# New prices and latencies in a kernel's order planner, and TensorE bound to the planner's order

## The chip, the cores and the metric

One core of one Trainium2 chip runs the kernel. The metric is the time of one execution in microseconds (us) on the device; the time given for a kernel is the median of its runs. TensorE is called PE in the profile, its weight loads PEld, VectorE DVE, ScalarE ACT, GpSimd POOL, and SyncE, which only issues DMAs, SP.

## The reference, cut to what matters

One layer of a decoder in float32, for a prompt of 512 tokens and 8 samples of one token each, 520 columns in all. Both groups use the same weights (d = 1024, FFN 2816).

```python
def hybrid_mixer(h, ...):
    proj = h @ w_in                              # 1024 -> 10016
    a_cols, s_cols, gate_a, gate_b = split(proj)
    for g in 3 groups:                           # (window, dilation) = (128,1), (512,4), (2048,16)
        q, k = rope(q), rope(k)                  # 8 heads of 64
        o[g], lse[g] = dilated window attention(q, k, v)
    o_a = sum_g softmax_g(lse) * o[g]
    o_b = rwkv7_time_mix(s_cols, ...)            # 16 heads of 64
    merged = sigmoid(gate_a) * (o_a @ w_proj_a) + sigmoid(gate_b) * (o_b @ w_proj_b)
    return merged @ w_out

def rwkv7_time_mix(p, prev, wkv0):
    xm = p + (shifted(p) - p) * mu_shift
    r, k, v, xw, xa, xg = split(xm)
    decay, a, gate = lora(xw), lora(xa), lora(xg)
    S_t = S * w_t + (S @ -kk_t) (kk_t * a_t)^T + v_t k_t^T     # scan over the tokens
    y_t = S_t @ r_t
    yn = group_norm(y) * gn_w + gn_b             # one group per head
    return (yn + bonus) * gate

x = x + hybrid_mixer(rms_norm(x), ...)
x = x + (silu(hn @ w_gate) * (hn @ w_up)) @ w_down             # hn = rms_norm(x)
y = rms_norm(x)
```

The new keys, values and RWKV states are outputs too.

## The kernel before

**Tiling.** Activations lie with channels on the partitions, in 8 blocks k of 128, and the 520 columns in two halves ("chunks") of 260. A product in float32 is made of three fast ones: each operand is split into a high part, rounded to the short format, and the rest (`whi` and `wlo` for weights; `hh`, `hl` for the normalised input, `hu`, `lu` for the first job's; `mh`, `ml` for the merged heads, `fh`, `fl` and `h2h`, `h2l` in the FFN), and high x high, low x high and high x low are added in PSUM. So a block of 128 output channels, a "job", is 8 x 3 matmuls of 128x128 weights and 260 columns for each half.

**Main stream.** `play` (L549) goes through the jobs: the attention's q, k, v and the RWKV's r, k, v of w_in, the gates (`hh`, `hl`), the projection of the attention's result (inputs `tw`, `k`, `ta`, `r`, `v`, used again as buffers; result summed up in `ga`), that of the RWKV's result (`OB`), w_out (`mh`, `ml`), the FFN. It fetches a weight block (`raw`), and ScalarE and VectorE split it into `whi` and `wlo`, one job ahead.

**Side streams.** The rest is generators that are spawned as their inputs appear: rotary turns (`turn`), attention (`heads`), the samples' attention and RWKV, and for each of 8 pairs of heads `pair` (the mixing and the LoRA products, tiles `LW`, `LA`, `lw`), `solve`, `turn_a` and `chain` (L1355). A chain goes through 8 blocks of 64 tokens, a "step" each: 64x64 products into `ch` from `VTr`, `GH` and the state `AR`; two ScalarE copies of `ch` into `GH`; 64x64 products `GH`, `KB`; a VectorE update of `AR`. Behind the last step come the outputs y (30 small products, of `GH` and of `AR`), copied into `KB` by ScalarE. Then follows the GroupNorm (L1424 to L1465): means `gm`, squares `gq` on ScalarE, a reciprocal root in ten VectorE operations (`rsy`, `rst`, L592), a product into `KB`, and four 128x128 transposes on TensorE, `ax<-ident,KB`. The last pair's normalisation is made of VectorE operations of 512 columns in place of the eight small ScalarE ones.

**What sets the order.** Python runs the generators. `Weave.run` (L433) picks at each point, by a model of time (`Clocks`, L226), a side stream whose awaited tiles are ready by the clock of TensorE, or else the main stream. `Unit.price` (L336) gives each operation's duration, and `Clocks.run` (L300) its start: after its inputs, its output tile's earlier users, and the work placed on its engine before. A stream stops at `yield tiles` until these are ready in the model. That gives the order in which the program is written:

```python
                p = self.price(op, outs, ins)
                if self.name == "PE":
                    ...
                    t = self.ck.run(self.name, outs, ins, p if self.ck.hot else 2 * p)
                ...
            if TIMED:
                self.tc.cur_priority = int(t * TIMED)
            r = f(*a, **k)
            return self.keep(r) if self.keep else r
```

With `TIMED = 0` and `PIN = 0` that order isn't the final one: the framework's scheduler sorts the instructions of each engine again, by its own estimates of when each can start and with the written order as priority. All instructions are issued through `Unit.__getattr__` (L353), so nearly all of them carry line L380 in the profile (L420 in the changed kernel); tiles tell them apart.

**The norms.** `norm2` (L1761) is spawned behind the last job of w_out, and `final` (L1822) behind the last job of the FFN. Each begins with `norm_r` (L608), whose first operations are matmuls with a column of ones: they sum `accf` (squares of x summed over the blocks) over the partitions. Neither has a `yield` ahead of them.

## Time and profile before

| | |
|---|---|
| time, median of 3 runs | 1314.66 us (1313.83 to 1316.19) |
| the profiled execution | 1316.53 us |
| its span in the trace | 1314.8 us, mean granted TensorE clock 0.983 |
| busy: TensorE, weight loads, VectorE, ScalarE, GpSimd | 1264.7, 1197.5, 843.7, 610.6, 175.0 us |
| start (0 to 33) | TensorE busy 23.98 of 33 us |
| mixer (33 to 858) | 795.07 of 825 us |
| output projection and FFN (858 to 1287) | 428.87 of 429 us |
| end (1287 to 1314.8) | 16.80 of 27.8 us |

A row of a timeline is start, duration (both us), engine, line, operation, tiles out<-in, tile of the array, form and count; in brackets stands the engine's idle time before it and what ended that. Matmuls overlap in the records, so that the distance between starts, not the duration, is what one costs. A group's row is engine, operation, tiles, form, count | busy us, mean ns of one | idle before and what ended it.

### The profile page before, as it was taken

To read this page: it belongs to the slowest core of one execution; us is meant where nothing else is said; L and a number is where in the kernel's file an instruction comes from. 1 tells how busy PE (TensorE), PEld (TensorE's weight loads), DVE (VectorE), ACT (ScalarE), POOL (GpSimd) and SP (SyncE) were. 2 spreads that over 40 slices of the span, in tenths; PEclk is the share of its full clock that TensorE was granted. 3 is DMA by queue.
4 is the path that set the end of the run, shared out by engine and by line. 5 is a ranking of instruction groups with operands and counts; after the bars stand their busy time and mean duration, and the time that the engine had idled before them with its cause. 6 is when DMAs were issued, how large, how long until landed. Compare 5 with 4: busy or idle time off the path is not lost.

```text
span 1314.8 us, 29468 instructions
## 1 busy us (share of the span) xinstructions
PE 1264.7 (96%) x11738; PEld 1197.5 (91%) x11738; DVE 843.7 (64%) x2221; ACT 610.6 (46%) x1554; POOL 175.0 (13%) x261
## 2 busy tenths in 40 slices
PE   7999999999989989999999999999999999999996
PEld 7998999989978878888888888999999999999996
DVE  6956866954869998886986665555843444332333
ACT  5244244366656656675785665334433232222220
POOL 1300100100223332121123122110200000000000
PEclk9999999999989999997999999999999999999998
DMA  6523654634245554543245454552222222223331
GB/s 215 158 94 96 213 178 146 221 112 172 69 131 136 152 147 141 143 156 97 77 139 168 123 175 157 182 192 85 81 97 97 97 89 89 97 93 89 89 101 65
DMA packets 92137, 169.48 MB, mean 129 GB/s; under 512 B 42416, under 2 KB 47568, under 8 KB 92000
## 3 DMA queue, kind: packets, MB, share of 16 engines
q1 hardware_dynamic: 60880, 102.46, 24.6%
q0 software_dynamic: 14512, 46.47, 11.5%
q10 hardware_dynamic: 16608, 18.68, 4.3%
q8 instruction: 92, 1.51, 0.5%
q14 instruction: 45, 0.37, 0.1%
HBM read 133.20 MB, written 27.94 MB: 123 GB/s over the span
## 4 chain that ended last, share of the span: by engine, by line
PE 64%; DVE 15%; issue 9%; DMA 6%; ACT 4%; POOL 1%; SPq 1%; ACTq 0%; DVEq 0%; POOLq 0%
PE mm L380 51%; PE ax L380 8%; PE ch L380 5%; DVE wlo L380 2%; DVE X L380 1%; DVE xt L380 1%; DMA fb<-FD 1%; DMA sw<-raw 1%; ACT KB L380 1%; DVE k L380 1%; DMA raw<-w_in 1%; SPq L380 1%; DVE raw L380 1%; DVE qk L380 1%; DVE GH L380 1%
## 5 line engine op out<-in xcount | busy, mean ns | idle before, releaser
L380 PE MATMUL mm<-hh,whi 128*128 128x260 f32 x1136 | 340.2, 299 | 0.8 <-ACT gt L380 0.8
L380 PE MATMUL mm<-hh,wlo 128*128 128x260 f32 x1136 | 325.4, 286 | 4.3 <-DVE wlo L380 4.3
L380 PE MATMUL mm<-hl,whi 128*128 128x260 f32 x1136 | 325.7, 287 | 0.0
L380 ACT CAST whi<-raw 128x1024 fp32r<-128x1024 f32 (+1 forms) x165 | 170.1, 1032 | 324.4 <-PE mm L380 290.6
L380 DVE TENSOR_TENSOR wlo<-raw,whi 128x1024 fp32r<-128x1024 f32 (+1 forms) x165 | 197.9, 1199 | 140.2 <-ACT whi L380 137.0
L380 PEld LDWEIGHTS mm<-hh,whi 128*128 128x128 f32 x1136 | 215.7, 190 | 13.3 <-issue 6.0
L380 PEld LDWEIGHTS mm<-hh,wlo 128*128 128x128 f32 x1136 | 215.4, 190 | 6.5 <-DVE wlo L380 5.8
L380 PEld LDWEIGHTS mm<-hl,whi 128*128 128x128 f32 x1136 | 215.5, 190 | 1.4 <-issue 0.2
L380 PE MATMUL mm<-h2l,whi 128*128 128x260 f32 x608 | 171.5, 282 | 0.0
L380 PE MATMUL mm<-h2h,wlo 128*128 128x260 f32 x608 | 171.4, 282 | 0.0
L380 PE MATMUL mm<-h2h,whi 128*128 128x260 f32 x608 | 171.4, 282 | 0.0
L380 PEld LDWEIGHTS mm<-h2h,wlo 128*128 128x128 f32 x608 | 114.5, 188 | 0.0
L380 PEld LDWEIGHTS mm<-h2l,whi 128*128 128x128 f32 x608 | 114.4, 188 | 0.0
L380 PEld LDWEIGHTS mm<-h2h,whi 128*128 128x128 f32 x608 | 114.4, 188 | 0.0
L380 PE MATMUL mm<-fh,wlo 128*128 128x260 f32 x388 | 109.6, 282 | 0.0
L380 PE MATMUL mm<-fh,whi 128*128 128x260 f32 x388 | 109.5, 282 | 0.0
L380 PE MATMUL mm<-fl,whi 128*128 128x260 f32 x388 | 109.5, 282 | 0.0
L380 PEld LDWEIGHTS mm<-fh,whi 128*128 128x128 f32 x388 | 73.1, 188 | 0.0
L380 PEld LDWEIGHTS mm<-fl,whi 128*128 128x128 f32 x388 | 73.0, 188 | 0.0
L380 PEld LDWEIGHTS mm<-fh,wlo 128*128 128x128 f32 x388 | 72.9, 188 | 0.0
L380 DVE TENSOR_TENSOR xt<-X,LT 128x60 f32<-128x60 f32 (+24 forms) x248 | 60.3, 243 | 3.6
L380 DVE TENSOR_TENSOR X<-X,xt 128x60 f32<-128x60 f32 (+24 forms) x248 | 57.6, 232 | 3.8
(390 smaller groups left out, 2588.8 us busy)
## 6 DMA issues: line engine op xcount, KB each, us to landing
raw<-w_in SPq DMA_DIRECT2D x77, 512.0 KB, 3.7
raw<-w_gate SPq DMA_DIRECT2D x22, 512.0 KB, 3.2
raw<-w_up SPq DMA_DIRECT2D x22, 512.0 KB, 3.2
raw<-w_down SPq DMA_DIRECT2D x16, 512.0 KB, 3.5
kt<-kcache POOLq DMA_DIRECT2D x24, 256.0 KB, 3.7
kt<-vcache POOLq DMA_DIRECT2D x24, 256.0 KB, 3.5
sw<-raw ACTq DMA_DIRECT2D x64, 65.0 KB, 3.6
GD<-gt ACTq DMA_DIRECT2D x16, 260.0 KB, 3.0
```

The source lines that it names most:

```text
L380: r = f(*a, **k)
```

## The change

It has three parts. First, the planner's figures: every engine's prices, the latency by which a result reaches another engine (`HOP`, by the writing engine, in place of 0.2 for all), DMAs, a surcharge on TensorE when the tile shape changes (`shift`), and rules by which a tile can't be used before its pool's predecessor is closed and its older users are through. Second, some `yield`s of side streams wait for more tiles, and one of `norm0` goes. Third, the starts that the planner gives to TensorE's instructions are kept in `ck.log`; at the end they are sorted by start and each is tied to the one before by a dependency without a semaphore. So TensorE's order is now the planner's; the other engines' instructions are sorted by the framework's scheduler as before. The matmuls are the same in number and shape.

```diff
-TIMED = 0
-PIN = 0
-L_SEM = 0.2
+HOP = {"PE": 0.2, "DVE": 0.04, "ACT": 0.04, "POOL": 0.1, "SP": 0.03}
...
 class Clocks:
     def last(d, engine, r=None):
-        t = 0.0
+        t, wake = 0.0, 0.2 if engine == "POOL" else 0.03
...
-                t = max(t, end + (late if by != engine else 0.0 if by == "PE" else 0.12))
+                t = max(t, end + (late + wake if by != engine else 0.0))
...
     def free(self, name, engine, r=None):
-        if name not in self.done and name in self.prev:
-            name, r = self.prev[name], None
-        return max(self.last(d.get(name, {}), engine, r) for d in (self.done, self.used))
+        n = self.prev.get(name)
+        return max([self.floor.get(name, 0.0), self.begun.get(self.order.get(name), 0.0)] +
+                   [self.last(d.get(name, {}), engine, r) for d in (self.done, self.used)] +
+                   [self.last(d.get(n, {}), engine) for d in (self.done, self.used)])
...
+    def shift(self, shape, op):
+        wide, t = shape == (128, 128), 0.0
+        if shape != self.shape:
+            t = 0.19 if wide else 0.09
+        elif wide and self.turned and op != "transpose":
+            t = 0.09
+        self.shape, self.turned = shape, op == "transpose"
+        return t
...
 class Unit:
-            return 0.06 + n / 1200
+            return (0.23 if op == "activation" else 0.18) + n / 1200 + (0.19 if more else 0)
         if self.name == "POOL":
-            return 0.25 + n / 480
+            return 0.2 + n / (310 if outs[0].dtype == FR else 600)
         if self.name != "PE":
-            return 0.07 + n / 960
+            if op == "tensor_tensor_scan":
+                return 0.155 + n / 480
+            return 0.155 + n / 960 + (0.05 if op == "scalar_tensor_tensor" else 0.08 if more else 0)
...
-        if ins[0].dtype == FR:
-            return max(0.054, n / 2400)
...
+        elif ins[0].dtype == FR:
+            p = max(0.065, 0.0115 + n / 2400)
...
+        return p + self.ck.shift((rows, cols), op)
...
-                t = self.ck.run(self.name, outs, ins, (2.7 if pool else 1.6) + kb / 360, 1.04 if pool else 0.45, 0.8)
+                t = self.ck.run(self.name, outs, ins, (3.4 if pool else 2.7) + kb / 300, 0.56 if pool else 0.36, 0.03)
...
-            if TIMED:
-                self.tc.cur_priority = int(t * TIMED)
             r = f(*a, **k)
-            return self.keep(r) if self.keep else r
+            self.ck.log[self.name].append((t, len(self.ck.log[self.name]), r.ins))
+            return r
...
     def norm0():
             split(hh[:, k], hl[:, k], t[:], (V, G)[k % 2])
-            yield (hl[:, k],)
...
     def gates2():
-            yield lo, st3, BANK
+            yield hi, lo, st3, rw["XGh"], rw["XGl"], rw["XS"], BANK
...
     def pair(p):
-        yield lo, BANK
+        yield hi, lo, LW, BANK
...
-        yield (BANK,)
+        yield LA, BANK
...
     def merge():
+            yield stat, BANK
...
     wv.run(play(jobs, more))
     fctx.close()
+    for log in (ck.log["PE"],):
+        log.sort(key=lambda x: x[:2])
+        for (_, _, a), (_, _, b) in zip(log, log[1:]):
+            tc.add_manual_dep(b, a.name, mybir.DependencyInfo(mybir.DependencyClass.NoSync, mybir.DependencyReason.DATA),
+                              reason="order")
```

Three places of the orders follow. The number behind a tile's name is that of its allocation; it differs between the kernels.

**The end of the mixer, TensorE.** Before, the four transposes of the last pair's GroupNorm (KB_9763) stand among the last gate products (`hh`, `hl`), and the output products (`OB`) come next; 77 gate products stand between that pair's y and these transposes.

```order
L380 MATMUL mm_11567<-hh,wlo_11408 128x260
L380 MATMUL mm_11567<-hh,whi_11407 128x260
L380 MATMUL mm_11567<-hl,whi_11407 128x260
L380 MATMUL ax_11590<-ident,KB_9763 128x128 x4
L380 MATMUL mm_11567<-hh,wlo_11408 128x260
L380 MATMUL mm_11625<-OB_11289,whi_11544 128x260 x2
L380 MATMUL mm_11625<-OB_11289,wlo_11545 128x260
L380 MATMUL mm_11625<-OB_11349,whi_11544 128x260 x2
```

Now there are no gate products left. Behind two bare steps of the last pair (KB_10239) stand the transposes of the pair before it (KB_9468), and behind them the last pair's y.

```order
L420 MATMUL ch_11441<-AR_9818 64x64 x2
L420 MATMUL ch_11441<-GH_9906,KB_10239 64x64
L420 MATMUL ch_11441<-GH_9907,KB_10239 64x64
L420 MATMUL ch_11492<-VTr_10292,GH_9906 64x64
L420 MATMUL ch_11492<-VTr_10292,GH_9907 64x64
L420 MATMUL ch_11492<-AR_9818 64x64 x2
L420 MATMUL ch_11492<-GH_9906,KB_10239 64x64
L420 MATMUL ch_11492<-GH_9907,KB_10239 64x64
L420 MATMUL ax_11516<-ident,KB_9468 128x128 x4
L420 MATMUL ch_11525<-GH_9906 64x64
L420 MATMUL ch_11525<-GH_9907 64x64
```

Fourteen more rows like the last two and one of `AR` (14 products) follow, and then `OB`. The gate products moved ahead by some 460 places.

**The second norm, TensorE.** `accf` holds the sums of squares; `mm<-mh` are the last products of w_out, `ch<-fh` and `ch<-fl` the first ones of the FFN. Before, thirty of the FFN's products stand ahead of the sum over the partitions:

```order
L380 MATMUL ch_12699<-fl,whi_12625 128x260
L380 MATMUL ch_12699<-fh,wlo_12626 128x260
L380 MATMUL ch_12730<-fh,whi_12625 128x260
L380 MATMUL ch_12730<-fl,whi_12625 128x260
L380 MATMUL ch_12730<-fh,wlo_12626 128x260
L380 MATMUL ax_12679<-ones,accf 104x1 x5
L380 MATMUL ch_12730<-fh,whi_12625 128x260
L380 MATMUL ch_12730<-fl,whi_12625 128x260
```

Now the sum comes directly behind w_out's last product:

```order
L420 MATMUL mm_12641<-mh,wlo_12563 128x260
L420 MATMUL mm_12641<-mh,whi_12562 128x260
L420 MATMUL mm_12641<-ml,whi_12562 128x260
L420 MATMUL mm_12641<-mh,wlo_12563 128x260
L420 MATMUL ax_12679<-ones,accf 104x1 x5
L420 MATMUL ch_12699<-fh,whi_12625 128x260
L420 MATMUL ch_12699<-fl,whi_12625 128x260
L420 MATMUL ch_12699<-fh,wlo_12626 128x260
```

So the sum moved ahead of the FFN's products. The same happens at `final`, where nine products of the down projection stood ahead.

**A GroupNorm near the mixer's end, VectorE and TensorE.** KB_8458 is a pair's y, `rst` and `rsy` its reciprocal root. On TensorE now:

```order
L420 MATMUL mm_11219<-r_10327,wlo_11093 128x260
L420 MATMUL mm_11219<-r_10328,whi_11092 128x260
L420 MATMUL mm_11219<-v_10332,whi_11092 128x260
L420 MATMUL mm_11219<-r_10328,wlo_11093 128x260
L420 MATMUL ax_11235<-ident,KB_8458 128x128 x4
L420 MATMUL mm_11244<-tw_10325,whi_11209 128x260
L420 MATMUL mm_11244<-k_10329,whi_11209 128x260
```

On VectorE now, up to the split of a weight block; five more steps of the root and `KB<-KB,rsy` come behind:

```order
L420 TENSOR_TENSOR rst_11122<-rsy_11121 128x8
L420 SCALAR_TENSOR_TENSOR ga_11077<-ga_11077,mm_11219 128x260
L420 SCALAR_TENSOR_TENSOR rst_11122<-rst_11122,gv_11035 128x8
L420 TENSOR_TENSOR OB_11568<-ys,OB_11568 128x8
L420 TENSOR_TENSOR OB_11575<-ys,OB_11575 128x8
L420 SCALAR_TENSOR_TENSOR rsy_11121<-rst_11122,rsy_11121 128x8
L420 TENSOR_TENSOR rst_11122<-rsy_11121 128x8
L420 TENSOR_TENSOR wlo_11314<-raw_11257,whi_11313 128x1024
```

VectorE before, for the same pair of heads (KB_8264):

```order
L380 TENSOR_TENSOR rst_10946<-rsy_10945 128x8
L380 SCALAR_TENSOR_TENSOR AR_8762<-AR_8762,PC_8570,ch_11048 128x64
L380 SCALAR_TENSOR_TENSOR rst_10946<-rst_10946,gv_10895 128x8
L380 SCALAR_TENSOR_TENSOR AR_9464<-AR_9464,PC_9243,ch_11088 128x64
L380 SCALAR_TENSOR_TENSOR rsy_10945<-rst_10946,rsy_10945 128x8
L380 SCALAR_TENSOR_TENSOR ga_10931<-ga_10931,mm_11076 128x260
L380 TENSOR_TENSOR KB_8264<-KB_8264,rsy_10945 128x512
L380 SCALAR_TENSOR_TENSOR AR_8762<-AR_8762,PC_8570,ch_11103 128x64
```

`ga<-ga,mm_11219` needs the product that stands last ahead of the transposes on TensorE, and stands on VectorE ahead of the operations that these transposes need. Before, no operation between the root's steps needed a product so late on TensorE: the last `ga` ahead of `KB<-KB,rsy` used mm_11076, which ended some 20 rows ahead of the transposes.

**The start, TensorE.** The products of the first job's two halves (mm_195 and mm_226) were mixed as slices of x came in; now the 24 of the first half stand ahead of the 24 of the second.

## The prediction

> **What bounds the kernel now.** I read the first part of the page, the busy time by stretch, TensorE's waits, and then the timeline where something is priced.

> ```profile
> span 1314.8 us, 29468 instructions
> ...
> PE 1264.7 (96%) x11738; PEld 1197.5 (91%) x11738; DVE 843.7 (64%) x2221; ACT 610.6 (46%) x1554; POOL 175.0 (13%) x261
> ```

> The columns of the stretches are length, busy time of PE, PEld, DVE, ACT and POOL, the granted clock, the DMA share and GB/s.

> ```profile
> 33.00:858.00 825.00, 795.07 (x7845) 729.65 (x7845) 622.01 (x1855) 463.95 (x1340) 159.14 (x238) 0.98 0.47 143
> 858.00:1287.00 429.00, 428.87 (x3589) 428.38 (x3588) 188.80 (x281) 126.58 (x179) 12.11 (x14) 1.00 0.30 98
> 1287.00:1314.80 27.80, 16.80 (x146) 16.29 (x144) 10.84 (x40) 0.84 (x2) 0.00 (x0) 0.80 0.23 77
> ```

> TensorE bounds it. From 858 on (output projection and FFN) it is idle for 0.13 us of 429, so an order can only lose there. All that can be won lies in the mixer, 33 to 858, where PE idles 30 us; beside that, its work costs more or less with the neighbours that the order gives it. VectorE is busy 75% of that stretch (622 of 825), so it is a second queue that a late operation has to get through.

> TensorE's waits (what waits, for what, total us, times, longest) have 21 rows from 7.6 down to 0.3 us, 41.8 in sum:

> ```profile
> PE mm L380 <- ACT whi L380: 7.6, 3, 7.1
> PE mm L380 <- DVE wlo L380: 5.1, 6, 1.4
> PE ch L380 <- ACT GH L380: 4.0, 4, 2.4
> ...
> PE mm L380 <- ACT hu L380: 1.7, 1, 1.7
> ...
> PE ax L380 <- DVE AR L380: 0.3, 1, 0.3
> ```

> The longest whi wait (7.1) is the first matmul's and the hu wait (1.7) is the start's too. The other 33 us are many waits of about 1 us on side streams: weights just split, steps of the RWKV chain, transposes of things not yet normalised.

> **The change, part by part.** The edits to prices, latencies and pool times issue no instruction; they count only through the order. The matmuls are the same ones. So I compare the two orders.

> *Fewer changes of tile shape.* A 64x64 step put among 128-wide matmuls costs more than its work:

> ```profile
> 795.36 0.28 PE L380 MATMUL mm<-v,whi 128*128 128x260 f32 x1
> 795.57 0.33 PE L380 MATMUL ch<-VTr,GH 64*64 64x64 f32 x4
> 795.74 0.28 PE L380 MATMUL ch<-AR 64*64 64x64 f32 x4
> 795.95 0.38 PE L380 MATMUL mm<-r,wlo 128*128 128x260 f32 x1
> 796.17 0.28 PE L380 MATMUL mm<-r,whi 128*128 128x260 f32 x1
> ```

> Starts of 128-wide matmuls in a run lie 0.12 apart (17.22 and 17.34 below). Into the 64x64 group it is 0.21 (+0.09); the first 128-wide one after it comes about 0.10 late, and the next 0.22 after that (another +0.10). In the orders, entries fall from 167 to 126, returns from 150 to 108, and changes between two small shapes rise from 116 to 144, at about 0.1 each: -41 x 0.09 - 42 x 0.205 + 28 x 0.1 = **-9.5 us**. That is the surest term: TensorE pays it whatever the others do. Half of it remains if the profile's spacing overstates it.

> *The mixer's waits.* With trace durations the plan places a chain step later. The step's rows are these, with those of the GroupNorm that follows a pair's chain:

> ```profile
> L380 ACT ACTIVATE GH<-ch,DN 64x64 f32<-64x64 f32 x128 | 39.6, 309 | 25.2 <-PE ch L380 20.9 <-DMA BVD<-tmp 1.8 <-issue 0.6
> ...
> L380 ACT ACTIVATE gq<-KB,gm 128x64 f32<-128x64 f32 x56 | 19.4, 346 | 0.7
> ...
> L380 DVE SCALAR_TENSOR_TENSOR AR<-AR,PC,ch 128x64 f32<-128x64 f32 x56 | 15.5, 278 | 20.3 <-PE ch L380 12.7 <-ACT gq L380 2.9 <-ACT VTr L380 2.3
> ...
> L380 ACT ACTIVATE KB<-ch 128x64 f32<-128x64 f32 x56 | 11.6, 235 | 3.9 <-PE ch L380 3.9
> ...
> L380 ACT ACTIVATION_READ_ACCUMULATOR gq<-KB,gm 128x1 f32 x56 | 10.5, 188 | 0.0
> ...
> L380 DVE SCALAR_TENSOR_TENSOR ga<-ga,mm 128x260 f32<-128x260 f32 x16 | 6.8, 423 | 3.3 <-PE mm L380 3.3
> ...
> L380 DVE TENSOR_TENSOR KB<-KB,gm 128x512 f32<-128x512 f32 x8 | 5.5, 688 | 3.0 <-ACT gq L380 2.9
> ...
> L380 DVE SCALAR_TENSOR_TENSOR rsy<-rst,rsy 128x8 f32<-128x8 f32 (+1 forms) x27 | 4.5, 166 | 0.4
> ```

> Between a step's first products and its second, which need two GH copies (2 x 0.309), stood 5 to 12 wide matmuls (0.6 to 1.4 us); now 12 to 42 (1.4 to 5.0). Counting in both orders the places where less than 2 us of TensorE work is left over beyond the bare durations of what is awaited, I find 104 before and 63 now. All 33 us go into the sum as removed, and the new waits come in again: at 33 / 104 = 0.32 us for a tight place, 63 of them would cost 20. Worked out singly, six GroupNorm transposes stand too early, for 12 us together. The largest is the one shown in VectorE's order: the transposes of KB_8458 come straight after the last product of mm_11219, but ahead of their last input VectorE has ga<-ga,mm_11219 (0.42), then two small adds and eight steps of the reciprocal root (0.2 each with the gap) and the product (0.69): 3.1 us, and more if the split wlo between them is late. The others, by the same rows, are 1.0 to 2.9. I add 6 for the rest: **-33 + 18**, the 18 between 5 and 40.

> *The mixer's tail.* Before, 77 gate matmuls (9.2 us at 0.12) stood between the last chain and the output product OB. Now they were used up earlier. Of the last two pairs, the first (KB_9468) has its y products, then only two steps of the other pair (three groups of small products each, 0.2 a group as above: 1.2 us), then its transposes. From y to the transposes that pair needs 8 x 0.235 (copies) + 8 x (0.346 + 0.188) (squares) + ten root steps at 0.2 + 0.69 = 8.9 us. So TensorE stands 7.7 us, with the other pair's y behind it in its queue. The two shared steps ahead of that leave it idle for some 3, and the second pair's normalisation (five wide operations at 0.69, root steps 2.0, copies 0.6: 6.0) is covered by 48 OB products (5.8) but for up to 1.5, with up to 3 more for changes of shape and stragglers: 11.5 to 16, I take **+14**.

> *The second norm.* From the timeline of before:

> ```profile
> 916.99 0.28 PE L380 MATMUL mm<-mh,wlo 128*128 128x260 f32 x1
> ...
> 917.31 0.43 DVE L380 TENSOR_TENSOR x<-x,mm 128x260 f32<-128x260 f32 x1 [1.87 <-PE mm L380]
> ...
> 918.82 0.63 ACT L380 ACTIVATE sq<-x 128x520 f32<-128x520 f32 x1
> ...
> 920.13 0.69 DVE L380 TENSOR_TENSOR accf<-accf,sq 128x520 f32<-128x520 f32 x1
> ...
> 920.97 0.99 PE L380 MATMUL ax<-ones,accf 128*104 128x1 f32 x10
> ```

> Thirty products of the FFN (3.6 us) covered the way from the last output product through x, sq and accf to the sum over channels. They now stand behind it, so TensorE waits: 920.97 - 917.11 = **+3.9**; 3 if ScalarE does sq ahead of the cast. The last norm loses its cover likewise:

> ```profile
> 1290.48 0.28 PE L380 MATMUL mm<-fh,lw 128*128 128x260 f32 x1
> ...
> 1291.84 0.23 PE L380 MATMUL ax<-ones,sq 128*65 128x1 f32 x2
> ```

> 1291.84 - 1290.60 = **+1.2**.

> *The start.* The first job was taken by both halves as slices of x came in; now all 24 products of the first half come first.

> ```profile
> 7.11 0.58 PE L380 MATMUL mm<-hu,whi 128*128 128x260 f32 x1 [7.11 <-ACT whi L380]
> ...
> 16.06 0.64 PE L380 MATMUL mm<-hu,whi 128*128 128x260 f32 x2
> 16.49 0.42 PE L380 MATMUL mm<-lu,whi 128*128 128x260 f32 x1
> 16.71 0.42 PE L380 MATMUL mm<-hu,wlo 128*128 128x260 f32 x1
> ...
> 17.22 0.28 PE L380 MATMUL mm<-hu,wlo 128*128 128x260 f32 x1
> 17.34 0.28 PE L380 MATMUL mm<-hu,whi 128*128 128x260 f32 x1
> ```

> ```profile
> 15.52 0.75 DVE L380 SCALAR_TENSOR_TENSOR lu<-xt,feat,hu 128x520 fp32r<-128x520 f32 x1
> ```

> The last slice is there at 16.27, when 32 of the 48 products had begun; now 24 + 2 would still wait, ten more, at 0.12 to 0.22 each: 1.2 to 2.2, less if the second half catches up. **+1.5**.

> *The clock.* In 594 to 627 the granted clock was 0.74 though TensorE was busy 32.6 of 33 us:

> ```profile
> 594.00:627.00 33.00, 32.58 (x278) 29.09 (x277) 21.60 (x81) 19.79 (x50) 5.31 (x7) 0.74 0.28 85
> ```

> At half clock a wide matmul takes 0.22, not 0.12 (rows at 16.49 and 17.22), so 26% of 33 us at a reduced clock cost about 8 us over the 0.12 pace, if each slowed product lost 0.1. Longer runs of wide products should spare some: **-3**, between -8 and +8. [...]

> **The sum.** The profiled run took 1316.5 us (its span is 1314.8). 1316.5 - 9.5 - 33 - 3 + 18 + 14 + 3.9 + 1.2 + 1.5 = 1309.6. The median of the runs shown, 1314.66, is 0.14% under the profiled run, so **1308 us**.

> **The rivals.** *VectorE and ScalarE don't follow* (slower). They are still sorted by the scheduler, and TensorE, now unable to take something else, stands behind each late hop: what the scheduler used to hide by moving ready products up is paid at each place. Its price is the wait per tight place. The sum breaks even when the 63 cost 25 us, 0.4 each; at 0.6 they cost 38 and, with the whole of the tail, the time is about **1328**. For it: VectorE busy 75%, the gate at KB_8458. Against: longer hops at most steps.

> *The plan is good* (much faster). Waits left in the body cost 3, not 18: 1294.6 on the profile's scale, **1293**. For it: most hops have over 2 us to spare. Against: the same plan puts the transposes and norms too early.

> *Waits only change places.* The 33 us come back whole, tail included: 1316.5 - 9.5 + 6.6 = 1313.6, **1312** by the medians; the order then does nothing but save changes of shape.

> [...]

> **How the numbers follow.** A measurement of this kernel can tell about 0.2%, 2.6 us, from no change: 1312.0 to 1317.3 is "same". Forecast 0.45, its own range 1299 to 1318 by its terms (0.35 faster, 0.09 same, 0.01 slower); good plan 0.20, faster; waits that change places 0.09 (0.04 faster, 0.05 same); the queues 0.19, slower; the clock 0.07 (0.06 slower, 0.01 same). Faster 0.59, same 0.15, slower 0.26. The range 1288 to 1327 leaves out the better part of the good plan below it (0.08) and the worse half of the queues above it (0.10).

> **What would show it.** Right: PE's busy time in the mixer falls by some 8 us with fewer small groups between wide ones; PE's waits name KB or rsy before ax transposes, with one of 5 to 9 us just ahead of OB; a wait of 3 to 4 us on accf opens the FFN; the middle of the FFN stays at 0.1 us idle. Wrong: the tail shows no wait over 4 us, or waits on GH and AR add up to more than 15 us, or wlo and whi (weights) become the largest rows, or the clock in the mixer drops below 0.96.

## The result and the profile after

The changed kernel takes 1375.46 us (median of 3 runs, 1373.37 to 1378.52) against 1314.66: ratio 1.0456, interval 1.0421 to 1.0491. It is slower by 61 us, outside the predicted range. The profiled run is the median one, with a span of 1373.7 us, 58.9 more than before.

The head of the page of the changed kernel and the granted clock in 40 slices:

```profile
span 1373.7 us, 29479 instructions
...
PE 1270.2 (92%) x11738; PEld 1209.0 (88%) x11738; DVE 845.5 (62%) x2221; ACT 611.7 (45%) x1554; POOL 167.5 (12%) x261
...
PEclk9999999999999899999999997899999999999997
```

The work is the same on every engine. TensorE's idle time is up from 50 to 104 us, and its busy time by 5.5 although there are fewer changes of shape: part of it ran at half clock (a granted clock of 0.50 over 103 us of the span by the trace's clock records, over 45 before).

Where the time went is read from landmarks with equal work ahead of them. The view by tile gives the first start of a group of products: 404 matmul records lie ahead of the first one with `hh`, 8118 ahead of the first with `mh` (w_out), 8810 ahead of the first with `h2h`. Columns: duration min/median/max in ns, first and last start in us. Before, then after:

```profile
L380 PE MATMUL mm<-hh,whi x1136: 277/283/787, 62.8 to 822.0; 128*128 128x260 f32 x188, 128*32 128x260 f32 x2
L380 PE MATMUL mm<-mh,whi x128: 278/282/288, 871.1 to 916.8; 128*128 128x260 f32 x128
L380 PE MATMUL mm<-h2h,whi x608: 278/282/288, 954.4 to 1171.6; 128*128 128x260 f32 x152
```

```profile
L420 PE MATMUL mm<-hh,whi x1136: 277/283/585, 76.3 to 791.1; 128*128 128x260 f32 x188, 128*32 128x260 f32 x2
L420 PE MATMUL mm<-mh,whi x128: 278/282/288, 922.4 to 968.5; 128*128 128x260 f32 x128
L420 PE MATMUL mm<-h2h,whi x608: 278/282/288, 1010.8 to 1228.1; 128*128 128x260 f32 x152
```

| stage | predicted | measured |
|---|---|---|
| start, to the first `hh` | +1.5 | +13.5 |
| mixer, to the first `mh` (-9.5 - 33 - 3 + 18 + 14) | -13.5 | 922.4 - 871.1 - 13.5 = +37.8 |
| w_out, second norm, to the first `h2h` | +3.9 | +5.1 |
| the rest, with the last norm | +1.2 | 58.9 - 56.4 = +2.5 |

By the timeline's brackets, TensorE's waits between the first `hh` and the first `mh`, in the mixer, went from 28.4 to 68.7 us. By kind, over the distances between all starts of TensorE, roughly: changes of shape -15.3 (75.9 to 60.6 us for entering a small shape and for the second wide product after it), long gaps +56 (42.5 to 98.5), wide products at half clock +12.2 (90 of them before, 221 after, about 0.1 each), the rest +6.

TensorE's waits after (what waits, for what, total, times, longest) are 95.2 us in 55, where before they were 41.2 in 41. The row of before that answers to the largest one comes first:

```profile
PE ax L380 <- DVE KB L380: 1.0, 2, 0.7
...
PE ax L420 <- DVE KB L420: 26.0, 6, 6.4
PE mm L420 <- DVE wlo L420: 10.0, 6, 5.6
PE ch L420 <- ACT GH L420: 8.0, 7, 3.1
PE mm L420 <- ACT whi L420: 7.6, 2, 7.3
PE ax L420 <- ACT QI L420: 4.3, 2, 3.5
PE ax L420 <- DVE X L420: 4.1, 1, 4.1
PE ax L420 <- DVE GH L420: 3.9, 3, 2.3
PE ax L420 <- DVE accf L420: 3.6, 1, 3.6
```

**The largest wait.** KB is a pair's y ahead of the GroupNorm's transposes. VectorE's timeline just before one of these (rst and rsy are the steps of the reciprocal root):

```profile
589.70 0.16 DVE L420 TENSOR_TENSOR rst<-rsy 128x8 f32<-128x8 f32 x1
589.77 0.68 DVE L420 TENSOR_TENSOR GH<-ax,wmask 128x512 f32<-128x512 f32 x1
590.38 0.15 DVE L420 SCALAR_TENSOR_TENSOR rst<-rst,gv 128x8 f32<-128x8 f32 x1
590.45 0.21 DVE L420 COPY AR<-ch 128x64 f32<-128x64 f32 x1
590.58 0.15 DVE L420 SCALAR_TENSOR_TENSOR rsy<-rst,rsy 128x8 f32<-128x8 f32 x1
...
590.66 0.68 DVE L420 TENSOR_REDUCE so<-kt 128x8 f32<-128x512 f32 x1
...
593.42 0.62 DVE L420 TENSOR_TENSOR KB<-KB,rsy 128x512 f32<-128x512 f32 x1
...
594.18 1.09 PE L420 MATMUL ax<-ident,KB 128*128 128x128 f32 x4 [6.38 <-DVE KB L420]
```

Between two root steps of 0.15 stands an operation of another stream of 0.2 to 0.7 (`so`, `kt` are the samples' attention). TensorE has nothing it may do meanwhile.

**The start.** A product with `wlo` waits for the split of its weights. ScalarE's part of it stands behind casts of hn, VectorE's behind operations on hn and hl and then those of the turns:

```profile
46.11 1.04 ACT L420 CAST whi<-raw 128x1024 fp32r<-128x1024 f32 x1
...
46.69 1.78 DVE L420 TENSOR_TENSOR sw<-sw,rope 128x520 f32<-128x520 f32 x1
...
50.30 1.21 DVE L420 TENSOR_TENSOR wlo<-raw,whi 128x1024 fp32r<-128x1024 f32 x1
...
51.56 0.58 PE L420 MATMUL mm<-hu,wlo 128*128 128x260 f32 x1 [5.62 <-DVE wlo L420]
```

`whi` was done at 47.15, but its `wlo` began 3.15 us later.

**The tail and the second norm.** The stretches of the changed kernel that hold them, and the last pairs' end (columns as in the prediction):

```profile
820.00:874.00 54.00, 36.26 (x394) 31.82 (x388) 24.52 (x78) 25.51 (x99) 8.09 (x15) 0.75 0.35 106
874.00:970.00 96.00, 91.68 (x754) 90.44 (x754) 55.10 (x94) 32.59 (x45) 11.19 (x21) 1.00 0.41 141
970.00:978.00 8.00, 5.39 (x34) 5.40 (x35) 4.34 (x14) 1.17 (x3) 0.00 (x0) 0.79 0.21 66
```

```profile
860.84 0.48 PE L420 MATMUL ch<-GH,KB 128*64 128x64 f32 x4 [1.07 <-ACT GH L420]
866.27 1.11 PE L420 MATMUL ax<-ident,KB 128*128 128x128 f32 x4 [4.95 <-DVE KB L420]
867.31 1.98 PE L420 MATMUL ch<-GH 128*64 128x64 f32 x32
869.22 1.76 PE L420 MATMUL ch<-AR 64*64 64x64 f32 x28
870.91 0.76 PE L420 MATMUL mm<-OB,whi 128*128 128x260 f32 x2
```

```profile
972.61 1.08 PE L420 MATMUL ax<-ones,accf 128*104 128x1 f32 x10 [3.60 <-DVE accf L420]
...
974.05 0.42 PE L420 MATMUL ch<-fh,whi 128*128 128x260 f32 x1
...
974.27 0.42 PE L420 MATMUL ch<-fl,whi 128*128 128x260 f32 x1
```

TensorE stands 17.7 us in the first stretch (before, in the 44 us ahead of OB: 3.6). Not all of that is the tail: 3.1 are a step's wait at 823.40 and 3.9 the GroupNorm gate at 836.23, with products of the projection behind both. From 847.7 to OB, where nothing but the last two pairs is left, it is 10.3. There the clock was at half (0.50 in the records from 851.0 to 871.5): a pair's 60 products of y take 3.60 us (867.31 to 870.91) and those of the pair before 3.45, and took 2.04 in the kernel before (from 792.11). Behind the wait on accf the products come 0.22 apart: half clock too (0.50 from 973.9 to 977.3).

### The profile page after: what moved, and what is told of

It reads as the page before. It is cut to its first block, busy times and chain, and to the rows that moved or that the text cites. A ratio compares the mean times of both kernels' runs of the same rounds, so it can differ in the third digit from the quotient of the medians.

```text
span 1373.7 us, 29479 instructions
## 1 busy us (share of the span) xinstructions
PE 1270.2 (92%) x11738; PEld 1209.0 (88%) x11738; DVE 845.5 (62%) x2221; ACT 611.7 (45%) x1554; POOL 167.5 (12%) x261
## 3 DMA queue, kind: packets, MB, share of 16 engines
q0 software_dynamic: 14512, 46.47, 11.5%
## 4 chain that ended last, share of the span: by engine, by line
PE 56%; issue 16%; DVE 15%; DMA 6%; ACT 3%; POOL 2%; SPq 0%; DVEq 0%; ACTq 0%; POOLq 0%
PE mm L420 46%; PE ax L420 7%; PE ch L420 4%; DVE wlo L420 2%; DMA fb<-FD 2%; DVE X L420 1%; DVE xt L420 1%; DVE qk L420 1%; DVE KB L420 1%; DMA raw<-w_in 1%; DVE sw L420 1%; DMA tmp<-OBD 1%; POOL kt L420 1%; DVE AR L420 1%; DVE kt L420 1%
## 5 line engine op out<-in xcount | busy, mean ns | idle before, releaser
L420 DVE TENSOR_TENSOR xt<-X,LT 128x60 f32<-128x60 f32 (+24 forms) x248 | 57.5, 232 | 3.8
```

## The experiments

Three theories. **P**: tied to the planner's order, TensorE stands wherever the plan called a tile ready too early; the scheduler of before had put ready products ahead. **R**: the new plan is at fault, tied or not. **Q**: the plan would do, but VectorE and ScalarE, which are still sorted by the scheduler, put other work ahead.

| kernel | tied | median us | ratio to before, interval | waits, us |
|---|---|---|---|---|
| before | no | 1314.66 | | 41.2 |
| changed | yes | 1375.46 | 1.0456, 1.0421 to 1.0491 | 95.2 |
| new plan, untied (e1) | no | 1335.3 | 1.0128, 1.0074 to 1.0182 | 55.6 |
| old plan, tied (e2) | yes | 1375.96 | 1.0469, 1.0442 to 1.0496 | 86.6 |
| three engines tied (e3) | yes | 1371.48 | 1.042, 1.039 to 1.045 | 87.0 |
| GroupNorm 5 us later (e5) | yes | 1355.2 | 1.0291, 1.0266 to 1.0317 | 78.3 |
| second norm waits (e4) | yes | 1369.85 | 1.0453, 1.0395 to 1.051 | 88.6 |
| first norm's yield back (e6) | yes | 1363.52 | 1.0392, 1.0337 to 1.0447 | 84.7 |
| these three (e8) | yes | 1346.06 | 1.0258, 1.021 to 1.0306 | 69.2 |
| these three, untied (e9) | no | 1331.41 | 1.0145, 1.0097 to 1.0193 | 50.7 |
| three and sg (e13) | yes | 1343.4 | 1.024, 1.0173 to 1.0307 | 68.9 |
| new yields alone (e10) | no | 1315.12 | 1.0041, 1.0008 to 1.0074 | 45.5 |
| new prices alone (e11) | no | 1329.15 | 1.0143, 1.0072 to 1.0214 | 52.1 |
| old plan, sg later (e12) | no | 1329.29 | 1.0135, 1.0074 to 1.0196 | 46.7 |
| old plan, GroupNorm later (e14) | no | 1310.57 | 0.9982, 0.995 to 1.0014 | 37.0 |
| old plan, TURNS 5 (e15) | no | 1318.43 | 1.0045, 1.0011 to 1.0079 | 47.6 |
| old plan, WARM 0.6 (e16) | no | 1335.85 | 1.017, 1.011 to 1.023 | 47.0 |
| new prices, TURNS 5 (e17) | no | 1317.69 | 1.0053, 1.0019 to 1.0086 | 43.6 |

The waits are those of the profiled run, which need not be the median one: that of e1 took 1321.79. The kernels ran on three chips, and each ratio is to runs of the kernel before on the same chip, with medians of 1315.6 (e1, e2, e3, e5), 1313.7 (e4, e6, e8, e9) and 1311.2 to 1312.3 (the others).

**Untie the new plan (e1); tie the old one (e2); tie three engines (e3).**

```diff
-    for log in (ck.log["PE"],):
+    for log in ():                                              # e1
+    for log in (ck.log["PE"], ck.log["DVE"], ck.log["ACT"]):    # e3
-PIN = 0                                                         # e2, on the kernel before
+PIN = 1
```

`PIN` keeps TensorE in the order in which the program is written; that is also the order of the planner's starts, since the planner never puts a matmul ahead of an earlier one.

> The changed kernel with its prices and yields, but without the dependencies that tie TensorE's order. Theory P (TensorE, tied to the planner's order, stands where the scheduler would have moved ready products up): 1308 to 1320 us, no wait of TensorE on KB over 1.5 us, waits in all 35 to 50 us. Rival R (the new plan itself is at fault: fewer products between GroupNorm and output, steps bunched at the end): 1345 us or more, with the KB waits still there.

> The kernel before, its old prices and yields, with TensorE tied to the order in which the planner writes. Theory P: slower than before by more than the change was, 1385 to 1430 us, since the old prices call tiles ready earlier still. Rival R: within 10 us of before, 1305 to 1325.

> The changed kernel with VectorE and ScalarE tied to the planner's order as well. Theory Q (the plan is fit for TensorE, but VectorE and ScalarE, sorted by another estimate, put other work ahead of what TensorE waits for): the KB waits fall from 26 to below 8 us and the time to 1310 to 1335. Rival (the planner's durations are too short, whatever the queues do): 1365 to 1400, with the KB waits above 15 us. More than 1400 would say that tying costs on these engines too.

The tie costs 40 us on the new plan (1375 - 1335), 15 on the one with three edits below (1346 - 1331) and 61 on the old one: P has the larger part. The mixer's waits say the same: 68.7 us with the tie and 36.1 without it on the new plan, 68.0 with it and 28.4 without it on the old one. It isn't all: e1 came out above what P said, with 20 us left over, and so did its waits, 55.6, and its longest wait on KB, 3.0. Its profiled run, the fastest, loses 7.1 us up to the first `hh` and none in the mixer; the three slower runs have the same instructions and a mean clock of 0.971 to 0.978 in place of 0.985. And e2 missed from the other side: tied, the old plan took no longer than the new one. But it has norm0's yield, and so an earlier first `hh` (64.4, not 76.3), while its mixer took 854.3 us against 846.1. With that yield put back (e6 below), the new plan is by the ratios the better one of the two when tied, 1.0392 against 1.0469, with intervals that just touch. In e3 the KB row went from 26.0 to 2.4, as Q said. The time did not follow, since other rows took its place:

```profile
PE mm L420 <- DVE wlo L420: 20.0, 11, 8.9
PE mm L420 <- ACT hu L420: 8.4, 2, 7.2
PE ax L420 <- ACT tw L420: 7.7, 2, 4.3
...
PE mm L420 <- ACT OB L420: 6.1, 1, 6.1
```

Q is right for the place and wrong for the sum: the planner's order for VectorE is late elsewhere, above all with weights.

**Take single waits out of the tied order (e5, e4, e6, all three: e8, and a fourth: e13).**

```diff
-        yield y, BANK                                  # e5: GroupNorm's transposes
+        yield (lambda: ck.at(y) + 5.0), BANK
...
+        yield ff["acc"], BANK                          # e4: norm2
         banks = yield from norm_r(ff["xp"], [ff["acc"]], slice(0, NT), TB, "f")
...
             split(hh[:, k], hl[:, k], t[:], (V, G)[k % 2])
+            yield (hl[:, k],)                          # e6: norm0, as before the change
...
-        yield g, BANK                                  # e13: transposes of sg
+        yield (lambda: ck.at(g) + 4.0), BANK
```

> The changed kernel with one edit: the GroupNorm's transposes are planned 5 us after the planner's clock calls their input ready. If the KB waits are a cost of their own, they fall from 26 to below 8 us and the time by 14 to 24, to 1351 to 1361. If they only take the place of waits that come next in the same streams (GH, OB, wlo), the time stays within 6 us of 1375.

> The changed kernel, still tied, with one edit: the second norm waits in the plan for accf, so that products of the FFN are written ahead of its sum over the partitions. If waits in a tied order add up one by one: the 3.6 us wait on accf goes and the time falls by 3 to 5, to 1370 to 1372. If the FFN's start then waits for its own weights or inputs: no change.

> The changed kernel, still tied, with the yield in the first norm put back that the change removed. Theory: that edit, not the tie, makes the 5.6 us wait on wlo at 51 us (the kernel without the tie has one of 7.6 there, the old plan tied has none), since eight blocks of hn and hl now stand ahead of the weight split on VectorE: the wait falls below 1.5 and the time by 4 to 8, to 1367 to 1371. Rival: the wait is one for weights from memory and stays; no change.

> The changed kernel, still tied, with three edits at once: GroupNorm transposes planned 5 us later, the first norm's yield back, the second norm waiting for accf. If each tied wait is paid by itself: 20 + 5.6 + 3.6 = 29 us less, 1342 to 1350. If the waits hide each other or the next ones grow: above 1355.

> The tied kernel with three edits (GroupNorm later, both norms) and the transposes of sg 4 us later as well. If tied waits are paid one by one, the 5.7 us wait on xt ahead of sg goes: 4 to 8 us less than the 1346 of the three edits, 1338 to 1342. If it only lets the next late tile come first: 1343 to 1349.

Tied waits are paid about one by one. In e5 the KB row fell to 3.3 and the time by 20.3; in e4 the wait on accf went, and the stage from the first `mh` to the first `h2h` shrank from 88.5 to 83.9: the 3.6 of the wait and 1.0 more, by my estimate that of its half-clock stretch (3.41 us in the changed kernel); the time fell by 5.6, which the intervals (1.0453 against 1.0456) don't resolve. In e6 the first `hh` product starts at 64.9 in place of 76.3, and the time falls by 11.9, more than expected: the edit in norm0 had cost 11 of the 13.5 us of the start. All three give 29.4, less than their sum of 37.8: each shifts what follows, and e6 had taken part of the KB waits with it (14.2 left). The fourth edit freed the transposes of sg, but the next product at that place waited as long; its 2.7 us lie within what the intervals leave open. VectorE's and TensorE's rows there with three edits, and with four:

```profile
464.54 0.69 DVE L420 TENSOR_TENSOR oo<-oo,fb 128x512 f32<-128x512 f32 x1 [5.51 <-DMA fb<-FD]
...
466.40 0.59 PE L420 MATMUL ax<-ident,sg 128*16 128x128 f32 x2 [5.68 <-DVE xt L420]
```

```profile
459.14 0.69 DVE L420 TENSOR_TENSOR oo<-oo,fb 128x512 f32<-128x512 f32 x1 [5.24 <-DMA fb<-FD]
...
461.01 0.56 PE L420 MATMUL ax<-LW,lwh 128*128 128x260 f32 x1 [5.71 <-DVE xt L420]
```

VectorE was late as a whole there, not with one tile, and not because it was busy: it stood 5.5 and 5.2 us itself, for a DMA that its next operation needed, with everything else behind it in its queue. Moving one gate let the next one show. Against the changed kernel, waits and time fall together: -39.6 and -40.2 (e1), -16.9 and -20.3 (e5), -6.6 and -5.6 (e4), -10.5 and -11.9 (e6), -26.0 and -29.4 (e8).

**Without the tie: where are the other 20 us (e9 to e12, e14 to e17)?** e9 is e8 untied, e10 takes the new yields alone (without norm0's) into the kernel before, e11 the new figures alone. The others edit the old plan without touching a price, or the new figures' TURNS:

```diff
-        yield g, BANK                                  # e12: sg, on the kernel before
+        yield (lambda: ck.at(g) + 4.0), BANK
...
-        yield y, BANK                                  # e14: GroupNorm, on the kernel before
+        yield (lambda: ck.at(y) + 3.0), BANK
...
-TURNS = 4                                              # e15 on the kernel before, e17 on e11
+TURNS = 5
-WARM = 0.65                                            # e16
+WARM = 0.6
```

> The same three edits, without the tie. Theory P: with the order left to the scheduler the GroupNorm and second norm edits matter little, and only the first norm's 7.6 us wait goes: 5 to 10 us under the new plan without the tie (1335), so 1322 to 1330, still 0 to 15 above before. Rival: the new plan's loss without the tie lies elsewhere, and the time stays at 1330 to 1340.

> The kernel before (old prices, no tie) with only those yields of the change that wait for more tiles (gates, pairs, merge), the first norm as before. Theory: the yields aren't what makes the new plan slow without the tie: 1308 to 1320 us. Rival: they delay the side streams, 1325 or more.

> The new prices, latencies and pool times alone: no tie, and all yields as before. Theory: the new figures hold the side streams back, the gate products run out before the chains, and the scheduler can't mend it: 1324 to 1340, with waits of 3 us or more on OB or GH just ahead of the output product. Rival: the prices are harmless without the tie, 1308 to 1320.

> The kernel before with one edit: in the samples' RWKV the transposes of sg are planned 4 us later, the two longest waits of the mixer there (2.7 and 3.2 us on sg and sd, one step of VectorE's each). If waits are paid one by one: 1307 to 1312. If the changed order shifts everything behind it: anywhere within 8 us of before.

> The kernel before with the GroupNorm transposes planned 3 us later, no tie, nothing else. If the old plan is one good draw among many: 1318 to 1332. If the loss of the new plan belongs to its prices: within 6 us of before.

> The kernel before with TURNS 5 in place of 4: the main stream may be kept waiting 5 us, not 4, by side streams. One good draw: 1318 to 1332. Prices: within 6 us of before.

> The kernel before with WARM 0.6 in place of 0.65, the share of wide products below which the main stream is taken first. One good draw: 1318 to 1332. Prices: within 6 us of before.

> The new prices alone, untied, with TURNS 5. If the loss belongs to the prices: 1324 to 1340 again. If plans scatter by 15 us whatever the prices: it can come out anywhere from 1310 to 1345, and below 1320 would show that the prices as such cost nothing.

Untied, the three edits change little (e9 against e1: 4 us, within their intervals). That is less than P said (1322 to 1330): the start got shorter (first `hh` at 61.2, in e1 at 69.9), but the loss lies elsewhere, as the rival had it. The yields are nearly innocent (+4). The new figures alone cost 18 us in e11, but 5 with another TURNS (each against the runs of before on the same chip). Two edits of the old plan that have nothing to do with prices cost 18 (e12: sg and sd fell from 5.9 to 1.1, and three waits on svd of 7.8 together took their place; all waits rose by only 5.5) and 24 (e16: only 6 us more of waits, but some 190 wide products at half clock in place of 90 in its profiled run, the slowest), two others -2 and +6. The bounds set ahead for these four were missed by e12 and e16, which lie above them all; e14 came out like the kernel before, as the prices at fault would have it, and e15 at the lower end of the range for one good draw. So untied plans scatter by some 25 us, and the kernel before is near the good end of that. Half clock has a large part in it: by the mean clocks (0.9865 for the kernel before on that chip, 0.9775, 0.979 and 0.974 for e11, e12 and e16) I estimate at most 12 of 18, 10 of 18 and 16 of 24 us, if at full clock that work would take half the time (wide products lie 0.22 apart at half clock and 0.12 at full). Whether the new figures also cost something of their own stays open: against the old ones they cost 18 with TURNS 4 (e11) and nothing with TURNS 5 (e17 1317.69, e15 1318.43). No version here is shown to beat the kernel before: e14's interval holds 1.

## Why the prediction was wrong, point by point

**The step that failed** is the one on the mixer's waits: "all 33 us go into the sum as removed", with 18 for new ones. What a tied order does to waits I had priced by a mean of the order before (0.32 us for a tight place). But that order came from a scheduler that could put ready products ahead of a late tile; without that, each lateness is paid in full. The term was -33 + 18 + 14 = -1 for the waits of the mixer with its tail; they rose by 40, from 28.4 to 68.7 (all waits: by 54). The runs show the cause by tying the old plan (mixer's waits 68.0, time +61) and by untying the new (36.1, time -40). Without the tail, the waits measured are 58 for the 63 tight places, 0.9 each.

**GroupNorm's gates** were the right place: the sum had 12 for six of them, and the five ahead of the tail measured 6.4, 1.9, 5.8, 3.1 and 3.9, together 21. The one shown in the order (KB_8458, forecast 3.1 or more) took 3.9. The largest was mis-sized because I counted only a few operations between the root's steps; VectorE's queue held foreign work there, as the timeline at 590 shows. "I add 6 for the rest" was the worst number: the mixer's other waits, on wlo, GH, QI, X, ta, tw, v and more, come to 37 (68.7 - 21.1 - 10.3).

**The start** was sized by the mixing of two halves alone, +1.5. I never costed the removed yield of norm0; it moved eight normalisations ahead of a weight split on VectorE and cost 11 us (e6).

**The tail** was right in kind and too large: +14 of standing, 10.3 measured. Its transposes waited 5.0 for the 7.7 forecast, and nothing stood ahead of the second pair's. Its terms come to 10.7 to 15.2, not to 11.5 to 16. Half clock then cost some 3 us on the products of y, which no term of the sum had. **The norms** were right as waits: 3.6 for 3.9; at `final` the wait is 0.97 for 1.2. Each also cost a stretch at half clock (0.50 for 3.41 us, from 973.9 and from 1349.4), so that the two stages came to +5.1 and +2.5. (The waits of before add up to 41.2, not 41.8, so the 33 are 32.4.)

**Changes of shape** were right in kind and too small: -15.3 for -9.5.

**The clock** had the wrong sign: -3 forecast, +12 measured. The -3 was my estimate: no run shows that longer runs of wide products spare the clock. In the changed kernel's trace each wait of 3 us or more behind the first product (nine of 3.1 to 6.4 us outside the tail), and the bare tail, came with half clock, 0.50 in the records. Shorter waits did so at five places and didn't at others, four of them of 1.7 to 2.3 us. The mean granted clock went from 0.983 to 0.963, and between the first `hh` and the first `mh` to 0.958, just below the 0.96 that the prediction names as a sign of being wrong. The low clock at 594 had been read with the waits ahead of it left out: TensorE was busy for 1.90 of the 3.35 us up to 593.85.

**The rivals.** The first one, VectorE and ScalarE not following, is what happened, at 0.19 where it deserved the most; its price stopped at 0.6 us for a tight place (1328), and the clock, to which the chances gave 0.07 without a cost read from a run, came on top of it, with the +12 us above.

## What to carry to other kernels

Fixing an engine to a planned order turned the lateness of the other queues into its idle time here: TensorE's waits rose by 54 us and the time by 59, with half clock (+12.2) and the saved changes of shape (-15.3) nearly in balance. Before fixing an order, take from the trace how late the tiles really are, with the foreign work and the waits for DMAs in the other engines' queues, and give the plan that slack; better durations alone don't supply it. And when the order is free, judge a change of plan against the scatter of plans: single edits moved this one by -2 to +24 us.

## What the runs showed of the hardware

**Half clock while TensorE is busy.** In the changed kernel, 22 wide products in a row ran 0.22 apart though TensorE didn't stand meanwhile. The clock had fallen behind a wait, though. The stretch ahead and the stretch itself (third column from the right: the clock, 1.00 and 0.50), and rows of both:

```profile
424.34:427.75 3.41, 1.74 (x27) 1.58 (x27) 0.00 (x0) 3.38 (x8) 0.00 (x0) 1.00 0.68 172
427.77:434.55 6.78, 6.78 (x40) 6.76 (x39) 6.42 (x20) 3.05 (x9) 3.52 (x4) 0.50 0.58 162
```

```profile
426.01 0.63 PE L420 MATMUL ax<-bsel,tmp 128*64 128x2 f32 x16 [1.78 <-ACT ta L420]
...
427.49 1.68 PE L420 MATMUL ax<-kw,st 128*64 128x4 f32 x16
...
430.34 0.42 PE L420 MATMUL mm<-hh,whi 128*128 128x260 f32 x1
430.56 0.42 PE L420 MATMUL mm<-hl,whi 128*128 128x260 f32 x1
```

```profile
593.90:610.90 17.00, 17.00 (x101) 14.95 (x100) 10.81 (x30) 6.49 (x15) 4.70 (x6) 0.50 0.28 84
```

That the small products kept it low was not tested. In the changed kernel the fifteen falls lie whole multiples of 3.413 us apart (at 21.57, 48.88, 294.64 us and so on: 8 and 72 of them between the first three). e1's four runs, with the same instructions, took from 1321.8 us at a mean clock of 0.985 to 1338.1 at 0.973; what made their clocks differ was not tested.

**VectorE beside GpSimd.** An operation with a median of 0.21 us took 2.50 while GpSimd worked on tensors:

```profile
504.90 2.50 DVE L420 TENSOR_TENSOR X<-X,xt 128x64 f32<-128x64 f32 x1
505.38 0.95 POOL L420 TENSOR_TENSOR AR<-AR,PC 128x448 f32<-128x448 f32 x1
506.27 2.16 POOL L420 TENSOR_TENSOR GH<-GH,DN 64x512 f32<-64x512 f32 x2
...
509.38 0.22 PE L420 MATMUL ax<-T,GH 32*32 32x32 f32 x2 [4.10 <-DVE X L420]
```

Of the 496 tensor operations between X and xt, 17 took over 0.45 us; all 17 overlap a GpSimd tensor operation, where 26 of the 496 do. That the overlap itself slowed them was not tested. TensorE's 4.10 us wait stood behind this one and the next on xt, which took 0.95. The planner's prices have no term for such an overlap.
